# A decoder block's output projection as seven products of blocks instead of eight, in a second pass over all tokens

## The chip, the cores and the metric

The kernel runs on one core of a Trainium2 chip. The time is the device time of one execution in microseconds (us); the number compared is a median over runs.

## The reference

The kernel computes a whole hybrid decoder block for 2048 tokens of width 1024 behind 16 learned meta tokens: a norm, one wide input projection, gated linear attention, latent attention, two branch projections, a gated merge, and the output. Only the end matters here:

```python
        y_b = (o_b * jax.nn.silu(m_z)) @ mla_proj[l]

        merged = jax.nn.sigmoid(gate_gla) * y_a + jax.nn.sigmoid(gate_mla) * y_b
        h = h + merged @ w_out[l]
    out = rms_norm(h, final_norm_g)
    return out[:, N_META:]
```

`y_a` times its gate is stored earlier in the kernel as `ma`. All values are float32. A product in float32 is made of three products of parts: each operand is split into hi (a rounded copy, made by ScalarE) and lo (operand less hi), and hi x hi, hi x lo and lo x hi are summed in PSUM by `mm3` (lines 44 to 47).

## The kernel before

The engines are TensorE (PE; PEld is its weight load), VectorE (DVE), ScalarE (ACT), GpSimd (POOL) and SyncE (SP), from whose queue all the transfers start. The program is written with a tile framework: pools of buffers are opened on the left or right end of SBUF, a tile waits for a buffer of its pool and tag, and the framework orders the instructions of each engine by when it takes them to be ready and, among those, by their place in the program. So the order in the trace isn't quite that of the text.

The stages are: the input projections (`phase_ab`, which already makes most of them by seven products of blocks for eight), the linear attention between them, the branch projection of the linear attention (`GlaProj`), the latent attention (`phase_c`) and the class `Output` (line 1530), which ends the kernel.

`Output` works in eight rounds `t` of 256 tokens. A round has two halves.

The merge: for each `mo` of eight blocks of 128 output columns, eight `kc` times three products of 128x256 go to `acc` (`product`, line 1562). They take `wp_hi`, `wp_lo` (columns `m` of `mla_proj`, loaded in round 0 by `load_w` in two halves of 256 KB through two raw buffers, split by `load_columns`, and kept) and `ob_hi`, `ob_lo` (attention output, transposed; `load_ob`, line 1577, loads each piece `kc` through one of two raw buffers, ACT rounds it, POOL subtracts). There are 12 buffers of each of these parts, 8 in use. ACT makes the sigmoid of a gate piece `gm` in three steps, DVE multiplies `acc` by it and adds `ma`, and the sum is split into `mg_hi`, `mg_lo`.

The projection: for each of two blocks of 128 tokens and each half of the 1024 columns, eight `kc` times three products of 128x512 go to `oacc`, from the round's `mg` parts and the parts of `w_out` (`wo_hi`, `wo_lo`, loaded and split in round 0 by `load_wo`, line 1601, and kept). DVE adds the row block of `x`, ACT squares with a sum, `rsqrt_cols` gives the scale and DVE scales both halves, which SP stores.

The first two `mo` of round 0 (`first`, line 1552) already run beside the end of the latent attention, with weights and `ob` loaded by `early` (line 1545); that end is the transposes `p_tp` of attention rows, the sums `o_acc` and a last product `po`. The rest of the weights of both kinds arrive during round 0. `main` opens its pools of weights `d_wb` and pieces `d_io` on the left end, where the latent attention held its constants, those of `po` among them; its rows and transposed parts lay on the right end.

## Time and profile before

| | us |
|---|---|
| median of 3 runs | 2585.53 |
| lowest, highest | 2579.38, 2586.53 |
| the profiled execution, its own time | 2587.8 |
| its span, first to last instruction | 2586.1 |
| mean granted clock of TensorE, as a share of 2.4 GHz | 0.996 |

The profile is of one execution. A page of it lists the busy time of each engine; windows give the same for chosen stretches, in us from the span's start; groups by line give counts, busy time and the mean duration of one instruction; timelines give single instructions: start, duration, engine, line, operation, output<-inputs, shape, count, and in brackets the idle time before it and what ended that. The duration of a matmul reaches from its start to the modelled end of its results, and neighbours overlap; the distance of two starts is the pace.

### The profile page before, as it was taken

How to read it: one execution, taken by the hardware profiler on the slowest of the kernel's cores; microseconds unless marked ns; L12 is line 12 of the kernel's file. 1: busy time of each engine (PE TensorE's matmuls, PEld its weight loads, DVE VectorE, ACT ScalarE, POOL GpSimd, SP SyncE). 2: the span in 40 equal slices, each digit the busy share in tenths (PEclk: the TensorE clock that was granted, in tenths of full speed). 3: DMA queues.
4: the chain of work that ended last, by engine and by line, in shares of the span. 5: the costliest groups of instructions: out<-in, count | busy, mean ns of one | idle time of the engine just before them, and what ended most of it. 6: DMA issues, size and time to landing. Idle time of an engine off the chain costs nothing.

```text
span 2586.1 us, 42507 instructions
## 1 busy us (share of the span) xinstructions
PE 2523.7 (98%) x14873; PEld 2234.2 (86%) x14873; DVE 1604.6 (62%) x3910; ACT 1343.8 (52%) x3202; POOL 325.4 (13%) x333
## 2 busy tenths in 40 slices
PE   7999999999999999999999999999999999899998
PEld 7998887878998888888877889999999999799997
DVE  7435878887624477786432387777776666543433
ACT  5323555774523275575354476655555555644342
POOL 2102332221301100000000010000000000211010
PEclk9999999999999999999999999999999999999999
DMA  5556776777466877777674332211111100643432
GB/s 145 164 158 230 254 243 208 245 243 238 116 185 208 247 227 243 242 238 231 225 231 146 111 119 67 65 46 42 46 38 34 33 18 25 195 150 115 126 109 70
DMA packets 302086, 392.59 MB, mean 152 GB/s; under 512 B 40464, under 2 KB 218944, under 8 KB 301872
## 3 DMA queue, kind: packets, MB, share of 16 engines
q1 hardware_dynamic: 301872, 389.88, 47.7%
q8 instruction: 117, 1.92, 0.3%
q14 instruction: 97, 0.79, 0.1%
HBM read 240.51 MB, written 149.25 MB: 151 GB/s over the span
## 4 chain that ended last, share of the span: by engine, by line
PE 75%; DVE 8%; ACT 7%; DMA 6%; issue 2%; POOL 2%; SPq 0%; DVEq 0%; POOLq 0%; ACTq 0%
PE acc L47 12%; PE acc L46 12%; PE acc L45 12%; PE p_tp L1383 4%; PE o_acc L46 3%; PE o_acc L45 3%; PE o_acc L47 3%; PE s L1331 2%; PE s L1335 2%; PE s L1333 2%; PE s L1334 2%; PE s L1332 2%; PE oacc L47 2%; PE oacc L46 2%; PE oacc L45 2%
## 5 line engine op out<-in xcount | busy, mean ns | idle before, releaser
L45 PE MATMUL acc<-t_hi,xp 128*128 128x512 f32 x640 | 254.6, 398 | 0.8 <-DVE y_lo L1120 0.8
L47 PE MATMUL acc<-t_hi,xp 128*128 128x512 f32 x640 | 250.3, 391 | 0.0
L46 PE MATMUL acc<-t_lo,xp 128*128 128x512 f32 x640 | 249.9, 390 | 0.0
L47 PE MATMUL acc<-w_hi,y_lo 128*128 128x296 f32 (+1 forms) x640 | 193.9, 304 | 4.8 <-DVE y_lo L187 4.8
L46 PE MATMUL acc<-w_lo,y_hi 128*128 128x296 f32 (+1 forms) x640 | 194.5, 304 | 3.3 <-DVE w_lo L187 3.0
L45 PE MATMUL acc<-w_hi,y_hi 128*128 128x296 f32 (+1 forms) x640 | 194.7, 305 | 2.5 <-ACT y_hi L186 1.6
L45 PE MATMUL acc<-y_hi,xp 128*128 128x512 f32 x480 | 192.0, 400 | 0.0
L47 PE MATMUL acc<-y_hi,xp 128*128 128x512 f32 x480 | 188.1, 392 | 0.0
L1350 ACT ACTIVATE row<-row,nm,sr 128x144 f32<-128x144 f32 (+15 forms) x128 | 167.3, 1307 | 39.6 <-DVE nm L1349 39.2
L46 PE MATMUL acc<-y_lo,xp 128*128 128x512 f32 x480 | 187.5, 391 | 0.0
L1386 DVE TENSOR_TENSOR p_lo<-p_tp,p_hi 128x512 fp32r<-128x512 f32 x224 | 150.3, 687 | 49.3 <-ACT p_hi L1385 46.6
L1385 ACT ACTIVATE p_hi<-p_tp 128x512 fp32r<-128x512 f32 x224 | 129.5, 595 | 98.3 <-PE p_tp L1383 97.5
L1383 PE MATMUL p_tp<-ident,row 128*128 128x128 f32 x1088 | 168.4, 273 | 0.0
L1337 DVE TENSOR_SCALAR_CACHE_REDUCE row<-s 128x388 f32<-128x388 f32 (+13 forms) x224 | 130.9, 585 | 59.4 <-PE s L1335 57.3
L45 PE MATMUL acc<-ob_hi,wp_hi 128*128 128x256 f32 x504 | 141.7, 281 | 3.8 <-ACT wp_hi L1092 2.9
L47 PEld LDWEIGHTS acc<-t_hi,xp 128*128 128x128 f32 x640 | 120.1, 188 | 25.8
L45 PEld LDWEIGHTS acc<-t_hi,xp 128*128 128x128 f32 x640 | 120.5, 188 | 24.5 <-issue 1.8
L47 PE MATMUL acc<-ob_hi,wp_lo 128*128 128x256 f32 x504 | 141.0, 280 | 0.1
L1383 PEld LDWEIGHTS p_tp<-ident,row 128*128 128x128 f32 x1088 | 128.8, 140 | 14.3 <-ACT row L1350 4.6
L46 PE MATMUL acc<-ob_lo,wp_hi 128*128 128x256 f32 x504 | 140.9, 280 | 0.0
L1331 PE MATMUL s<-kt_hi,q_hi 128*128 128x420 f32 (+16 forms) x352 | 139.5, 397 | 1.2 <-DVE mx L1340 1.2
L46 PEld LDWEIGHTS acc<-t_lo,xp 128*128 128x128 f32 x640 | 120.4, 188 | 22.2
(338 smaller groups left out, 7293.5 us busy)
## 6 DMA issues: line engine op xcount, KB each, us to landing
d_xp<-xp SPq DMA_DIRECT2D x80, 512.0 KB
xp<-d_xp SPq DMA_DIRECT2D x80, 512.0 KB
w_raw<-in_w_in SPq DMA_DIRECT2D x60, 512.0 KB
xt<-in_x SPq DMA_DIRECT2D x32, 512.0 KB
d_z<-c SPq DMA_DIRECT2D x32, 256.0 KB
z<-d_z SPq DMA_DIRECT2D x64, 128.0 KB
v_hi<-d_vh SPq DMA_DIRECT2D x64, 128.0 KB
v_lo<-d_vl SPq DMA_DIRECT2D x64, 128.0 KB
```

What stands on the lines that cost most here:

```text
L45: nc.tensor.matmul(out, a_hi, b_hi, start=start, stop=False)
L46: nc.tensor.matmul(out, a_hi, b_lo, start=False, stop=False)
L47: nc.tensor.matmul(out, a_lo, b_hi, start=False, stop=stop)
L1331: nc.tensor.matmul(sv, q_hi[:, js], kt_hi[:, a:b], start=True, stop=False)
L1332: nc.tensor.matmul(sv, q_hi[:, js], kt_lo[:, a:b], start=False, stop=False)
L1333: nc.tensor.matmul(sv, q_lo[:, js], kt_hi[:, a:b], start=False, stop=False)
L1334: nc.tensor.matmul(sv, qa[:, js], kst[:, a:b], start=False, stop=False)
L1337: nc.vector.tensor_scalar(row[:, a:b], sv, 1.0, None, op0=ALU.mult, op1=ALU.max, accum_out=mx[:, i:i + 1])
L1350: nc.scalar.activation(row[:, :w], row[:, :w], AF.Exp, bias=nm, scale=sr[:, 4 * t + j:4 * t + j + 1], accum_out=rl[:, j:j + 1])
L1383: nc.tensor.transpose(tp[:, i, r * P:(r + 1) * P], rws[r][:, M + k * P:M + (k + 1) * P], ident)
L1385: nc.scalar.activation(fl(p_hi), fl(tp), AF.Copy)
L1386: nc.vector.tensor_sub(fl(p_lo), fl(tp), f(fl(p_hi)))
```

## The change

The output stage becomes two passes over all the tokens. The first, `merge`, runs the merge of all eight rounds; merged values aren't split but stored to a new DRAM tensor `S.mg`, one store for each piece of 128x256, issued one `mo` later. The pools `d_wb` and `d_io` now open on the right end, `ma` has four buffers of its own. In rounds 1 to 4 the generator `blocks` loads the rows `kc` and `4 + kc` of `w_out`, forms the sums t1 to t4 of its four blocks (DVE and POOL) and splits y11, t1, t2, t3 and y21 into parts that stay in SBUF; t4 goes to DRAM. From round 5 pools for the operands of the second pass are open, and in the last round `ahead` makes the first three operands.

The second pass, `project`, runs over eight pairs of row blocks of 128 tokens. For each pair, `operands` loads the merged values in halves of both dimensions and forms seven operands (four of them by a sum or difference, two made by DVE, two by POOL), each split by ACT and DVE into one of four buffers. Seven products of four `kc` times three matmuls of 128x512 follow, with the right sides y11, t1, t2, t3, y21, t4, y22. Out of PSUM, ACT copies the first and DVE adds the others to the four quarters of the two output rows; POOL adds the quarters of `x`; ACT squares; `finish` scales and the stores follow one step later. t4 and y22 are loaded and split at the start of the second pass.

```diff
+        self.mg = [pool.tile([P, KC, 512], F32, name=f"d_mg{t}") for t in range(NT)]
+        self.t4 = pool.tile([P, KC // 2, 512], F32, name="d_t4")
...
+    def merge(self):
...
+        wb = self.right("d_wb", KC - 1)
+        io = self.right("d_io", 3)
+        mp = self.right("d_mg", 4)
...
+        self.T = {n: [tp.tile([P, KH, 512], F32R, name=f"o{n}_{e}") for e in ("hi", "lo")]
+                  for n in ("y11", "t1", "t2", "t3", "y21")}
...
+        tmp = Pools(self.tc)
+        self.wraw, self.sums = tmp("d_wr", 1), tmp("d_ws", 1)
+        stores = []
...
+            build = self.blocks(t - 1) if 0 < t <= KH else None
+            if t == KH + 1:
+                tmp.close()
+                self.operands_pools()
...
+                while len(stores) > 1:
+                    nc.sync.dma_start(*stores.pop(0))
...
-                mg.append(self.split(hp, ma, ("mg_hi", "mg_lo"), nc.vector))
...
-                    for kc in range(KC):
-                        hi, lo = mg[kc]
-                        mm3(nc, acc[n], hi[:, bs], lo[:, bs], wo[kc][0][:, ns], wo[kc][1][:, ns],
-                            kc == 0, kc == KC - 1)
-                    nc.vector.tensor_add(xt[:, ns], xt[:, ns], acc[n])
-                    nc.scalar.activation(y[:, ns], xt[:, ns], AF.Square, accum_out=ssq[:, n:n + 1])
...
+                stores.append((S.mg[t * W // 512][:, mo, t * W % 512:t * W % 512 + W], ma))
+                if build is not None and mo % 2:
+                    next(build, None)
+                if t == last and mo >= 2:
+                    self.ahead()
...
+    def halves(self, n, kc, src, lo_engine):
+        hi, lo = self.T[n]
+        self.nc.scalar.activation(hi[:, kc], src, AF.Copy)
+        lo_engine.tensor_sub(lo[:, kc], src, f(hi[:, kc]))
+    def blocks(self, kc):
+        nc, KH = self.nc, KC // 2
+        up, dn = (self.wraw.tile([P, D], F32, tag=n, name=n) for n in ("w_up", "w_dn"))
+        nc.sync.dma_start(up, self.wo[kc * P:(kc + 1) * P])
+        nc.sync.dma_start(dn, self.wo[(KH + kc) * P:(KH + kc + 1) * P])
+        y11, y12, y21, y22 = up[:, :512], up[:, 512:], dn[:, :512], dn[:, 512:]
+        t1, t2, t3, t4 = (self.sums.tile([P, 512], F32, tag=f"f{i}", name=f"f{i}") for i in range(4))
+        yield
+        nc.vector.tensor_sub(t1, y12, y11)
+        nc.vector.tensor_sub(t2, y22, t1)
+        nc.gpsimd.tensor_sub(t3, t2, y11)
+        nc.gpsimd.tensor_sub(t4, y21, t2)
+        self.halves("y11", kc, y11, nc.vector)
+        yield
+        self.halves("t1", kc, t1, nc.vector)
+        self.halves("t2", kc, t2, nc.vector)
+        yield
+        nc.sync.dma_start(self.S.t4[:, kc], t4)
+        self.halves("t3", kc, t3, nc.vector)
+        self.halves("y21", kc, y21, nc.vector)
+    def operands_pools(self):
+        xp, self.mraw, self.msum = self.left("o_x", 3), self.left("o_raw", 1), self.left("o_sum", 1)
+        self.xps, self.made = [xp] * 3, 0
+        self.ops, self.ready = self.operands(), []
+    def operands(self):
+        nc, KH = self.nc, KC // 2
+        def load(p, k):
+            raw = self.mraw.tile([P, KH, 2 * P], F32, tag=f"r{k}", name="m_raw")
+            nc.sync.dma_start(raw, self.S.mg[p // 2][:, k * KH:(k + 1) * KH, p % 2 * 2 * P:(p % 2 + 1) * 2 * P])
+            return raw[:, :, :P], raw[:, :, P:]
+        def parts(src):
+            t = self.xps[self.made % len(self.xps)].tile([P, 2, KH, P], F32R, tag="xp", name="xp")
+            self.made += 1
+            nc.scalar.activation(t[:, 0], src, AF.Copy)
+            nc.vector.tensor_sub(t[:, 1], src, f(t[:, 0]))
+            return t
+        def summed(tag, eng, op, a, b):
+            t = self.msum.tile([P, KH, P], F32, tag=tag, name=tag)
+            eng.tensor_tensor(t, a, b, op=op)
+            return t
+        for p in range(L // (2 * P)):
+            x11, x21 = load(p, 0)
+            x12, x22 = load(p, 1)
+            yield parts(x11)
+            s1 = summed("sa", nc.vector, ALU.add, x21, x22)
+            yield parts(s1)
+            s2 = summed("sb", nc.vector, ALU.subtract, s1, x11)
+            yield parts(s2)
+            yield parts(summed("sa", nc.gpsimd, ALU.subtract, x11, x21))
+            yield parts(x12)
+            yield parts(x22)
+            yield parts(summed("sa", nc.gpsimd, ALU.subtract, x12, s2))
...
+    def ahead(self):
+        if len(self.ready) < 3:
+            self.ready.append(next(self.ops))
+    def project(self):
+        nc, KH, NP = self.nc, KC // 2, L // (2 * P)
+        right = Pools(self.tc, "right")
+        tp, xo, op = right("o_t", 1), right("o_in", 4), right("o_row", 4)
+        yo, up, sm, cst = right("o_y", 3), right("o_u", 1), right("o_sm", 6), right("o_cst", 1)
+        wr = right("o_wr", 4)
+        self.xps.append(right("o_x2", 1))
+        for n in ("t4", "y22"):
+            self.T[n] = [tp.tile([P, KH, 512], F32R, name=f"o{n}_{e}") for e in ("hi", "lo")]
...
+        def product(right):
+            acc = self.pb.tile([P, 512], F32, tag="b", name="oacc")
+            while len(self.ready) < 4:
+                t = next(self.ops, None)
+                if t is None:
+                    break
+                self.ready.append(t)
+            t = self.ready.pop(0)
+            hi, lo = self.T[right]
+            for kc in range(KH):
+                mm3(nc, acc, t[:, 0, kc], t[:, 1, kc], hi[:, kc], lo[:, kc], kc == 0, kc == KH - 1)
+            return acc
+        def step():
+            now = [s for s in stores if s[0] <= 0]
+            stores[:] = [(n - 1, *s) for n, *s in stores if n > 0]
+            for _, dst, src in now:
+                nc.sync.dma_start(dst, src)
+            if later:
+                later.pop(0)()
+        def finish(p, h, o, ssq):
+            nc.vector.tensor_add(ssq[:, :1], ssq[:, :1], ssq[:, 1:])
+            rstd = rsqrt_cols(nc, sm, ssq[:, :1], 1, 1.0 / D)
+            y = yo.tile([P, D], F32, tag="y", name="y")
+            r0 = (2 * p + h) * P
+            for n in range(2):
+                ns = slice(n * 512, (n + 1) * 512)
+                nc.vector.scalar_tensor_tensor(y[:, ns], o[:, ns], rstd, fg[:, ns], op0=ALU.mult, op1=ALU.mult)
+                stores.append((1, self.out[r0:r0 + P, ns], y[:, ns]))
...
+            nc.scalar.activation(c11, product("y11"), AF.Copy)
+            step()
+            p5 = product("t1")
+            step()
+            u2 = up.tile([P, 512], F32, tag="u2", name="u2")
+            nc.vector.tensor_add(u2, product("t2"), c11)
+            nc.vector.tensor_add(c12, p5, u2)
+            nc.gpsimd.tensor_add(c11, c11, x11)
+            nc.gpsimd.tensor_add(c12, c12, x12)
+            step()
+            nc.vector.tensor_add(c21, product("t3"), u2)
+            nc.vector.tensor_add(c22, p5, c21)
+            nc.gpsimd.tensor_add(c21, c21, x21)
+            nc.gpsimd.tensor_add(c22, c22, x22)
+            if p + 1 < NP:
+                xs[p + 1] = rows(p + 1)
+            step()
+            nc.vector.tensor_add(c11, product("y21"), c11)
+            square(0, 0, c11)
+            square(1, 1, c22)
+            step()
+            nc.vector.tensor_add(c21, product("t4"), c21)
+            square(1, 0, c21)
+            later.append(lambda a=(p, 1, o[1], ssq[1]): finish(*a))
+            step()
+            nc.vector.tensor_add(c12, product("y22"), c12)
+            square(0, 1, c12)
+            later.append(lambda a=(p, 0, o[0], ssq[0]): finish(*a))
+            if p + 1 < NP:
+                step()
...
```

## Rows read from the trace of the kernel before

**Rows 1.** The page's list of engines: busy time, share of the span, instructions.

```profile
PE 2523.7 (98%) x14873; PEld 2234.2 (86%) x14873; DVE 1604.6 (62%) x3910; ACT 1343.8 (52%) x3202; POOL 325.4 (13%) x333
```

**Rows 2.** Windows by stage: busy time of each engine (x instructions), columns in first line.

```profile
core 0: us, PE busy (x) PEld busy (x) DVE busy (x) ACT busy (x) POOL busy (x), PEclk, DMA share, GB/s
2218.40:2256.61 38.21, 32.06 (x197) 26.20 (x198) 23.36 (x35) 27.11 (x56) 11.14 (x10) 1.00 0.81 248
2256.61:2268.60 11.99, 10.55 (x46) 8.07 (x46) 9.28 (x17) 8.20 (x24) 4.08 (x4) 1.00 0.64 198
2489.76:2512.46 22.70, 22.70 (x194) 22.65 (x194) 11.82 (x30) 11.20 (x31) 1.54 (x2) 1.00 0.41 122
2512.46:2534.26 21.80, 21.80 (x98) 18.02 (x98) 5.70 (x14) 6.13 (x17) 1.55 (x3) 1.00 0.25 79
...
2578.53:2586.10 7.57, 0.00 (x0) 0.00 (x0) 3.05 (x9) 1.13 (x4) 0.00 (x0) 0.75 0.19 69
```

**Rows 3.** Groups by line, end of the kernel: count | busy us, mean ns | idle.

```profile
L46 PE MATMUL oacc<-wo_lo,mg_hi 128*128 128x512 f32 x256 | 99.8, 391 | 0.0
```

**Rows 4.** Timeline of PE, first and last of 20 products in a row.

```profile
2485.06 0.39 PE L45 MATMUL oacc<-wo_hi,mg_hi 128*128 128x512 f32 x1
...
2489.37 0.39 PE L46 MATMUL oacc<-wo_lo,mg_hi 128*128 128x512 f32 x1
```

**Rows 5.** Timeline of SP's queue: weight loads of gla_proj, then of mla_proj.

```profile
1290.38 2.36 SPq L1080 DMA_DIRECT2D w_raw<-in_gla_proj  x2
...
1302.82 1.85 SPq L1080 DMA_DIRECT2D w_raw<-in_gla_proj  x2
...
2219.84 1.61 SPq L1080 DMA_DIRECT2D w_raw<-in_mla_proj  x2
...
2253.08 1.88 SPq L1080 DMA_DIRECT2D w_raw<-in_mla_proj  x2
```

**Rows 6.** Timelines of PE and ACT around the first merge.

```profile
2212.80 0.49 PE L1383 MATMUL p_tp<-ident,row 128*128 128x128 f32 x3
...
2217.97 0.40 PE L47 MATMUL po<-och,wv_lo 128*128 128x512 f32 x1
...
2218.46 1.15 ACT L1092 ACTIVATE wp_hi<-w_raw 128x512 fp32r<-128x512 f32 x2 [1.34 <-PE po L47]
...
2256.33 0.28 PE L47 MATMUL acc<-ob_hi,wp_lo 128*128 128x256 f32 x1
```

**Rows 7.** Timelines of ACT, SP, PE and POOL around one end of a merge.

```profile
2466.16 0.71 ACT L1568 ACTIVATE ob_hi<-ob 128x256 fp32r<-128x256 f32 x2
...
2467.40 1.20 SPq L1581 DMA_DIRECT2D ob<-d_ob  x2
...
2468.02 0.40 PE L45 MATMUL oacc<-wo_hi,mg_hi 128*128 128x512 f32 x1
...
2471.51 0.74 POOL L1569 TENSOR_TENSOR ob_lo<-ob,ob_hi 128x256 fp32r<-128x256 f32 x1 [0.46 <-ACT ob_hi L1568]
```

**Rows 8.** Timelines of POOL and DVE in the paired input projections.

```profile
211.63 1.30 POOL L432 TENSOR_TENSOR sb<-sa,w_raw 128x512 f32<-128x512 f32 x1
...
211.91 1.57 DVE L187 TENSOR_TENSOR xp<-w_raw,xp 128x512 fp32r<-128x512 f32 x1
...
515.38 0.69 DVE L187 TENSOR_TENSOR xp<-w_raw,xp 128x512 fp32r<-128x512 f32 x1 [1.27 <-ACT xp L186]
515.99 0.69 DVE L522 TENSOR_TENSOR u<-acc,c 128x512 f32<-128x512 f32 x1
...
521.17 1.30 POOL L432 TENSOR_TENSOR sa<-w_raw 128x512 f32<-128x512 f32 x1 [8.65 <-DVE xp L187]
...
521.54 0.42 DVE L827 TENSOR_TENSOR kt_lo<-kt,kt_hi 128x256 fp32r<-128x256 f32 x1
```

**Rows 9.** Windows of the paired projections, columns as in rows 2.

```profile
472.00:493.50 21.50, 21.27 (x114) 18.06 (x113) 20.41 (x48) 18.40 (x49) 4.96 (x5) 1.00 0.71 234
...
536.50:558.00 21.50, 20.35 (x106) 16.88 (x105) 18.68 (x41) 15.17 (x42) 4.47 (x4) 1.00 0.76 247
```

**Rows 10.** Timeline of DVE behind the last product.

```profile
2581.66 1.41 DVE L1652 SCALAR_TENSOR_TENSOR y<-xt,rs_y,fg 128x512 f32<-128x512 f32 x2
```

More of the change, by code (lines that the diff above doesn't have):

```diff
@@ L1586, in main @@
     def main(self):
+        self.merge()
+        self.project()
+        self.left.close()
+        self.psum.close()
+        self.psum_r.close()
+    def merge(self):
         nc, S, W = self.nc, self.S, self.W
         self.obp += [self.right("d_ob2", 4)] * 4
-        left, psp = self.left, self.psum
-        wb = left("d_wb", KC - 1)
-        io = left("d_io", 3)
-        hp = left("d_h", 10)
-        cst = left("d_cst", 1)
-        xo = left("d_x", 2)
-        sm = left("d_sm", 3)
-        self.pa.append(psp("d_pa2", 2, space=PSUM))
-        pb = psp("d_pb", 4, space=PSUM)
-        fg = cst.tile([P, D], F32, name="fg")
-        wo = []
-        def load_wo(kc):
-            if kc == 0:
-                nc.sync.dma_start(fg, self.fg.partition_broadcast(P))
-            raw = xo.tile([P, D], F32, tag="x", name="wo_raw")
-            nc.sync.dma_start(raw, self.wo[kc * P:(kc + 1) * P])
-            wo.append(self.split(cst, raw, (f"wo_hi{kc}", f"wo_lo{kc}"), nc.vector))
+        wb = self.right("d_wb", KC - 1)
+        io = self.right("d_io", 3)
+        mp = self.right("d_mg", 4)
+        tp = self.left("d_t", 1)
+        KH = KC // 2
+        self.T = {n: [tp.tile([P, KH, 512], F32R, name=f"o{n}_{e}") for e in ("hi", "lo")]
+                  for n in ("y11", "t1", "t2", "t3", "y21")}
+        self.pa.append(self.psum("d_pa2", 2, space=PSUM))
+        self.pb = self.psum("d_pb", 4, space=PSUM)
+        tmp = Pools(self.tc)
+        self.wraw, self.sums = tmp("d_wr", 1), tmp("d_ws", 1)
+        stores = []
+        last = L // W - 1
         for t in range(L // W):
```

60 lines of the change are left out of this document (37 added, 23 removed).

## The prediction

> **What bounds the kernel now.** The page's list of engines comes first: TensorE (PE) is busy for 98% of the span [rows 1], so only work taken off PE, or waits put on it, can count. The windows by stage then show which part of the output stage is full [rows 2]. In a later round the merge takes 22.70 us and the output projection 21.80 us, PE busy throughout; DVE is at about half in the one and a quarter in the other, DMA at 0.41 and 0.25. The start differs: from 2218.40 to 2256.61 PE is busy for 32.06 of 38.21 us and DMA share is 0.81. The list by line has 768 products into oacc, 256 on each of three lines [rows 3]. Their mean there is latency, not pace; the timeline gives the pace: 19 starts in 4.31 us, 0.2268 us each [rows 4].
>
> **What is removed.** Eight products of blocks become seven: 8 pairs x 7 x 4 x 3 = 672 products for 768. The 96 saved are worth 96 x 0.2268 = 21.8 us, one round's projection.
>
> Where does that leave the end? Before, first-round projection ends at 2268.60 and last at 2578.53: seven rounds, 309.9 us. Afterwards, what follows the first merge is seven merges and 672 products (152.4 us), again seven times 22.70 + 21.80. So the gain equals how much earlier the first merge is through than 2268.60, less new waits. In the kernel before its last product starts at 2256.33 [rows 6]; after it 12.0 us of projection remained [rows 2], the other 9.8 us having filled holes between arriving weights. With the first merge unchanged the gain is 12.0 us, not 21.8: the filler is lost.
>
> **The first merge.** It is paced by columns of mla_proj: two loads for each m, issued from 2219.84 to 2253.08, five intervals of 6.65 us [rows 5]. w_out's eight 512 KB loads no longer run among them. The nearest row without such company is the same loader on gla_proj, two intervals in 12.44 us, 6.22 each [rows 5]. From m=3 to m=7 are four intervals: 4 x 0.43 = 1.7 us earlier. Bounds: nothing, since blocks of w_out for round 1 may load early too, and 1.7.
>
> The chain's start may move. The first split of these weights waited for product po, begun last at 2217.97 [rows 6], as d_wb lay over attention constants on the left; on the right it lies over attention rows and parts, whose last transposes start at 2212.80 [rows 6]. Between 0 and 2218.46 - 2213.3 = 5.2 us; I take 2, since some of those parts are read until shortly before po.
>
> For filler PE has only round 1's first products. Four ob pieces can be ahead (12 slots, 8 in use): 12 products of 256 columns, 22.70 / 192 = 0.118 us each, 1.4 us for one accumulator and 5.6 for four. I take 1.4.
>
> Sum so far: 12.0 + 1.7 + 2.0 + 1.4 = 17.1 us.
>
> **What is added.** *Round boundaries, seven.* Pieces 4 to 7 of the next ob need slots that free only in the last mo. Their loads, split and POOL subtraction were hidden by the projection; now the next merge follows at once. In a boundary of before, the merge ended at 2468.02, the first two of these splits began at 2466.16, the next two loads at 2467.40, and the last subtraction, 0.74 us, at 2471.51 [rows 7]: 4.2 us after the end. PE needs that piece after 22 products, 2.6 us. So 1.7 us with no filler, and nothing if PE takes the next mo's pieces 0 to 5 first, as it filled holes in the start. I take 0.7 each, 5 us, bounds 0 and 11.9. SP queues other loads behind those that wait for a raw buffer; three gm and four ma buffers give the merge about 8 us of cover.
>
> *Through DRAM.* Merged values are stored and loaded, 1 MiB a round each way, with their waits on SP. A merge round then moves 4 MiB in 22.7 us, 185 GB/s, and 5.25 MiB, 243 GB/s, in the four rounds with blocks; the start ran at 248 [rows 2]. Cost nothing while a load has a buffer ahead; otherwise it appears in the boundaries above, which is why I don't take 0 there.
>
> *Making the sums.* Blocks of rounds 1 to 4 add 7 DVE operations of 0.69 us [rows 8], 5 ACT copies and 2 POOL subtractions to a round; DVE's 11.82 us of a merge [rows 2] rise by 4.8 at most (the splits of merged values leave), under PE's 22.70. Without that cover they would add some 5 us a round.
>
> *Handover.* Three operands are ready; t4 and y22, loaded and split after the merge pools close, are wanted after five and six products of 12 x 0.2268 = 2.72 us, 13.6 us later. I take 1 us, bounds 0 and 3 (a product).
>
> *The projection pass.* A pair takes 84 x 0.2268 = 19.05 us of PE. DVE does 7 splits, 2 sums and 7 additions from PSUM, spaced 0.60 us where DVE is full (515.38 to 515.99) [rows 8], 9.6 us; four scalings, 1.41 us for two [rows 10], 2.8; and 12 small operations of 0.16 to 0.2, 2.3: 14.7 us, 77%. POOL does 6 additions of 1.30 us, 7.8 [rows 8]. These collide: while POOL ran 1.30 us from 211.63, a DVE split with both inputs in SBUF, 0.69 us otherwise, took 1.57; a DVE subtraction from PSUM under the POOL row of 521.17 took its usual 0.42 [rows 8]. So only splits, sums, scalings and the small multiplications, some 9.2 us, exclude POOL. If half of POOL's six each cost DVE 0.9 us, DVE is at 17.4 of 19.05 us, 91%. In stretches of 21.5 us with DVE at 20.41 and 18.68, PE lost 0.23 and 1.15 [rows 9], but those wait on a recurrence too; four operands ahead cover about 8 us here. I take 0.2 a pair, 1.5 us; bounds 0 and, if nothing overlaps (22.5 us a pair), 28.
>
> The Trainium skill, "SBUF — State Buffer", section "Who interferes with whom", says that a DVE instruction with two SBUF inputs and a GpSimd one that reads SBUF shut each other out for a whole instruction. The trace agrees, 1.57 us for 0.69, and 0.42 where an input is in PSUM [rows 8]. By that rule alone a pair lies between 17.0 us, which leaves the sum as it is, and 22.5 us, the second rival.
>
> ACT has some 8 copies (two in 1.15 us [rows 6]) and four squares a pair, under 10 us of 19, costed at nothing.
>
> *End.* After the last product 7.57 us remain [rows 2]; the same chain stays, with the other row block's scaling beside it: 0.8 us, bounds 0 and 2.
>
> **Sum.** 17.1 - 5 - 1 - 1.5 - 0.8 = 8.8 us. The profiled execution took 2587.8 us (span 2586.1), so it would take 2579.0; the median of the three runs, 2585.53, is 2.3 below that execution, giving 2576.7 us.
>
> **Rivals.**
> 1. *Boundaries are not filled.* PE's order keeps mo after mo, so seven waits of 1.7 us stay: 17.1 - 11.9 - 3.3 = 1.9 us, 2583.6. Slower loads in a fuller DMA would take it to about 2592. For: nothing but the next mo can fill, and DMA nearly doubles. Against: in the start PE did take out-of-turn products whenever weights were late. 22%.
> 2. *VectorE and GpSimd bound the projection pass: slower.* Place: the 6 POOL additions a pair against splits and scalings. Price: up to 22.5 - 19.05 = 3.45 us a pair, 28 us in all; 17.1 - 6.8 - 28 = -17.7, 2603. It decides once POOL costs DVE over 4.3 us a pair (14.7 + 4.3 = 19.05), and turns the whole change slower at about 5.6. For: 0.9 to 1.1 us in single collisions. Against: 4.2 us of PSUM additions a pair can run beside POOL. 9%.
> 3. *A quick first merge.* Chain 5.2 us earlier, four accumulators of filler, boundaries filled: 12.0 + 1.7 + 5.2 + 5.6 - 1 = 23.5, 2562. 17%.
> That fewer products are not issued isn't open: the loops fix 672.
>
> **How the numbers follow.** The forecast has 52%, with 2570 to 2582 as its own range. Range for 8 in 10: 2563 (rival 3) to 2592 (rival 1's far end); rival 2 and part of rival 3 lie outside. A measurement here tells about 0.3%, 7.8 us, from no change, so the line is 2577.8. Faster: 37 of the forecast's 52 and rival 3's 17, 54%. Same: 15 from the forecast and 18 from rival 1, 33%. Slower: 4 from rival 1 and rival 2's 9, 13%.
>
> **What would show it.** Right: 672 products into oacc at 0.227 us; first merge through at about 2250; seven merges in 158 to 165 us with small PE gaps only at boundaries, ended by ob_lo or ob_hi; pairs of 19 to 19.3 us; 8 us behind the last product. Wrong: PE gaps of over 2 us at boundaries (rival 1); DVE over 95% in the projection pass with PE waiting for xp (rival 2); first merge before 2246 (rival 3) or after 2257, which would undo the first terms.

## The result, and the profile after

The changed kernel takes 2624.14 us (median of four runs, 2622.8 to 2625.3), the kernel before 2584.46 us beside it: a ratio of 1.0156, 95% interval 1.0139 to 1.0174. It is slower by 40 us, where 2576.7 us had been forecast with a range of 2563 to 2592. The profiled execution has a span of 2623.3 us against 2586.1, so 37.2 us are to be found.

The page's list of engines, after [rows 1]:

```profile
PE 2528.3 (96%) x14777; PEld 2235.0 (85%) x14777; DVE 1660.4 (63%) x3970; ACT 1368.0 (52%) x3222; POOL 409.6 (16%) x389
```

96 products fewer, and PE is busy 4.6 us longer. Windows by stage (columns as the first line says): rest of the first merge, seven merges, projection pass, tail [rows 2].

```profile
core 0: us, PE busy (x) PEld busy (x) DVE busy (x) ACT busy (x) POOL busy (x), PEclk, DMA share, GB/s
2218.40:2250.50 32.10, 23.49 (x157) 21.82 (x158) 10.50 (x21) 18.48 (x42) 10.46 (x10) 0.89 0.70 207
2250.50:2448.20 197.70, 177.45 (x1337) 170.66 (x1336) 78.89 (x146) 98.47 (x240) 55.13 (x60) 0.93 0.58 181
2448.20:2612.80 164.60, 156.34 (x674) 125.38 (x672) 121.98 (x244) 65.18 (x158) 67.99 (x47) 1.00 0.47 154
2612.80:2623.30 10.50, 0.01 (x1) 0.00 (x0) 5.14 (x17) 2.18 (x8) 0.00 (x0) 0.69 0.27 101
```

The second line holds the result: seven merges take 197.7 us, where 158 to 165 were forecast, and the granted clock, 1.00 in every stage of [rows 2] that had products, is 0.93 over these 198 us. Against the terms of the forecast:

| stage | forecast | measured | late by |
|---|---|---|---|
| first merge through (the first round's projection was, before: 2268.60) | 2250 | 2250.5 | 0 |
| seven merges | 158 to 165 (309.9 - 152.4 = 157.5, and 5 for boundaries) | 197.7 | 35 |
| handover and 672 products | 154.9 (152.4 + 1 + 1.5) | 164.6 | 10 |
| behind the last product | 8.4 | 10.5 | 2 |

From the kernel before: -18.1 + 40.2 + 12.2 + 2.9 = 37.2 us, the difference in span.

PE's waits after 2250 us (line waiting, what it waited for: us in total, times, longest):

```profile
PE acc L45 <- ACT ob_hi L1574: 11.1, 8, 2.5
PE oacc L45 <- ACT xp L1695: 8.1, 6, 1.5
PE acc L46 <- POOL ob_lo L1575: 7.9, 15, 1.5
PE acc L45 <- ACT wp_hi L1094: 0.8, 1, 0.8
PE oacc L47 <- DVE xp L1696: 0.2, 1, 0.2
```

In the merges nearly all of them are for pieces of the next round's ob. The 40.2 us can be split by the distance from one product's start to the next, less a product's pace of 0.118 us. Distances over 0.5 us are waits, 25.1 us. Distances near 0.213 us, half the clock, make some 9 us. Those of 0.3 to 0.5 us, in which short waits and half the clock mix, make 4 us, and a pace of 0.120 in place of 0.118 makes the remaining 2.4. By boundary, from the first to the seventh, the loss is 4, 11, 6, 8, 5, 2 and 4 us; the sums are made in the merges that end at the second to the fifth. Windows behind the second boundary and the fourth, and at the seventh, columns as above:

```profile
2283.00:2287.00 4.00, 2.00 (x8) 1.49 (x7) 3.67 (x4) 3.17 (x8) 3.40 (x3) 0.50 0.53 167
2287.00:2291.00 4.00, 3.07 (x15) 2.78 (x14) 2.13 (x3) 2.72 (x7) 2.70 (x3) 0.50 0.54 184
...
2347.00:2351.00 4.00, 4.00 (x20) 4.00 (x21) 1.50 (x3) 3.01 (x8) 2.55 (x3) 0.56 0.73 217
2351.00:2355.00 4.00, 4.00 (x36) 4.00 (x35) 0.98 (x3) 1.01 (x3) 0.47 (x1) 1.00 0.65 191
...
2424.00:2428.00 4.00, 1.31 (x6) 0.91 (x7) 0.00 (x0) 2.35 (x6) 1.46 (x2) 1.00 0.61 192
```

After the waits of the first five boundaries the granted clock falls to 0.50, the level of 1.2 GHz, for 27 us in all; at the sixth and seventh it stays at 1.00, although PE is busy for 1.31 of 4 us in the last line. In the line from 2347 PE is busy throughout at 0.56 and starts 20 products, where the next line, at 1.00, starts 36. So the clock cost between 9 us, the starts 0.213 us apart, and 13 us with the mixed ones.

How a boundary comes late, from the timelines of SP, POOL, ACT and PE at the second one, the end of the first of the seven merges:

```profile
2262.04 0.40 SPq L1631 DMA_DIRECT2D ma<-d_ma  x1
...
2264.65 1.75 POOL L1668 TENSOR_TENSOR f<-w_dn,f 128x512 f32<-128x512 f32 x1
...
2266.43 0.32 SPq L1674 DMA_DIRECT2D d_t<-f  x1
...
2268.24 0.42 SPq L1628 DMA_DIRECT2D gm<-d_gm  x1
...
2271.66 0.42 ACT L134 ACTIVATE gm<-gm 128x256 f32<-128x256 f32 x1 [4.34 <-DMA gm<-d_gm]
...
2272.43 0.40 ACT L1574 ACTIVATE ob_hi<-ob 128x256 fp32r<-128x256 f32 x1
...
2274.50 2.40 SPq L1587 DMA_DIRECT2D ob<-d_ob  x2
...
2276.56 0.63 ACT L1653 ACTIVATE oy_hi<-w_up 128x512 fp32r<-128x512 f32 x1 [0.82 <-DMA w_up<-in_w_out]
...
2279.02 0.71 ACT L1574 ACTIVATE ob_hi<-ob 128x256 fp32r<-128x256 f32 x2
...
2279.47 0.38 PE L45 MATMUL acc<-ob_hi,wp_hi 128*128 128x256 f32 x1 [2.06 <-ACT ob_hi L1574]
2279.50 1.60 POOL L1575 TENSOR_TENSOR ob_lo<-ob,ob_hi 128x256 fp32r<-128x256 f32 x2 [2.94 <-ACT ob_hi L1574]
```

SP stands from 2262.4 to 2266.4 at the store of t4, until POOL has made it; gm is requested late; ACT stands 4.34 us at that gm, and ob's rounding is behind it. The next requests of ob wait for one of two raw buffers (2.40 us for two requests), and ACT stands at w_up. In every queue something stands ahead of ob's pieces, so there is a candidate in each: SP, ACT, POOL, two raw buffers. Which of them was it?

### The profile page after: what moved, and what is told of

Same layout as the page of the kernel before. It is cut to its first block, busy times and chain, and to the rows that moved or that the text cites. A ratio compares the mean times of both kernels' runs of the same rounds, so it can differ in the third digit from the quotient of the medians.

```text
span 2623.3 us, 42759 instructions
## 1 busy us (share of the span) xinstructions
PE 2528.3 (96%) x14777; PEld 2235.0 (85%) x14777; DVE 1660.4 (63%) x3970; ACT 1368.0 (52%) x3222; POOL 409.6 (16%) x389
## 4 chain that ended last, share of the span: by engine, by line
PE 63%; DVE 11%; DMA 10%; ACT 7%; issue 5%; POOL 3%; SPq 1%; POOLq 0%; DVEq 0%; ACTq 0%
PE acc L46 11%; PE acc L47 11%; PE acc L45 11%; PE p_tp L1385 4%; PE o_acc L46 3%; PE o_acc L45 3%; PE o_acc L47 2%; PE s L1333 2%; PE s L1337 2%; PE s L1335 2%; PE s L1336 2%; PE s L1334 2%; DMA ob<-d_ob 1%; DMA m_raw<-d_mg 1%; DMA gm<-d_gm 1%
## 5 line engine op out<-in xcount | busy, mean ns | idle before, releaser
L1339 DVE TENSOR_SCALAR_CACHE_REDUCE row<-s 128x388 f32<-128x388 f32 (+13 forms) x224 | 130.9, 585 | 59.4 <-PE s L1337 57.3
L45 PE MATMUL acc<-ob_hi,wp_hi 128*128 128x256 f32 x504 | 149.2, 297 | 19.1 <-ACT ob_hi L1574 11.1
L46 PE MATMUL acc<-ob_lo,wp_hi 128*128 128x256 f32 x504 | 149.8, 298 | 8.2 <-POOL ob_lo L1575 7.9
L47 PE MATMUL acc<-ob_hi,wp_lo 128*128 128x256 f32 x504 | 147.4, 294 | 1.6 <-POOL wp_lo L1095 1.4
L1438 POOL TENSOR_TENSOR rb<-rb,mz 128x512 f32<-128x512 f32 x32 | 42.0, 1313 | 644.2 <-DMA rb<-d_rl 337.9
```

Source lines behind the costliest of these rows:

```text
L45: nc.tensor.matmul(out, a_hi, b_hi, start=start, stop=False)
L46: nc.tensor.matmul(out, a_hi, b_lo, start=False, stop=False)
L47: nc.tensor.matmul(out, a_lo, b_hi, start=False, stop=stop)
L1339: nc.vector.tensor_scalar(row[:, a:b], sv, 1.0, None, op0=ALU.mult, op1=ALU.max, accum_out=mx[:, i:i + 1])
```

## The experiments

The names: A, two raw buffers and 12 part buffers; B, POOL; C and E, SP's queue; D, the sums of w_out's blocks; G, ob's pieces as a whole; F and H are told with their runs. The table gives, for each profiled execution, the merges (from the last product of po to the last product into acc, since the stage starts at 2213 to 2221 us), the pass from there to the last product into oacc, and the time as a whole. By the kernel before's rows the merges would be 38.4 us for the first [rows 6] and seven times 22.70 [rows 2], 197.3. Kernels whose merges are the changed kernel's show 229.4, 233.3 and 234.3 us: the framework orders them anew each time, and up to 5 us mean nothing. The kernel before was timed beside each kernel, with medians of 2584.5 to 2588.7 us, so times are better compared by the last column.

| kernel | merges | pass | time | ratio to before, interval |
|---|---|---|---|---|
| the changed kernel | 229.4 | 164.4 | 2624.1 | 1.0139 to 1.0174 |
| four raw buffers | 223.1 | 163.8 | 2618.6 | 1.0107 to 1.0143 |
| ob asked for earlier | 230.2 | 164.7 | 2625.4 | 1.0133 to 1.0173 |
| sums on VectorE | 225.8 | 165.5 | 2622.0 | 1.0120 to 1.0160 |
| sums later in the text | 233.2 | 165.4 | 2632.0 | one run |
| t4 stored later | 229.1 | 164.7 | 2627.0 | 1.0135 to 1.0165 |
| t4 later, four raw buffers | 223.3 | 165.9 | 2614.0 | 1.0086 to 1.0120 |
| sums behind the merges | 218.1 | 199.5 | 2647.6 | one run |
| stores from ScalarE's queue | 239.7 | 164.4 | 2633.5 | 1.0162 to 1.0194 |
| stores from GpSimd's queue | 235.8 | 163.7 | 2624.5 | 1.0127 to 1.0161 |
| six ma buffers | 230.5 | 166.0 | 2624.6 | 1.0133 to 1.0166 |
| ob loaded once | 199.3 | 171.3 | 2603.8 | one run |
| sums in half steps | 230.8 | 166.2 | 2622.1 | one run |
| half steps, 16 part and 4 raw buffers | 222.5 | 165.3 | 2614.0 | 1.0097 to 1.0131 |
| the same, second r1 | 222.8 | 161.0 | 2610.5 | 1.0079 to 1.0109 |
| the same, five gm buffers | 231.1 | 161.2 | 2619.5 | 1.0104 to 1.0138 |
| ob once, sums behind the merges | 190.8 | 206.7 | 2628.3 | one run |
| second r1 | 233.3 | 162.5 | 2623.0 | 1.0124 to 1.0158 |
| second r1, no additions of x | 234.3 | 155.2 | 2617.5 | 1.0102 to 1.0136 |

**Single links of the boundary.** First the raw buffers:

```
-        self.obr = self.right("d_obr", 2)
+        self.obr = self.right("d_obr", 4)
```

> Four raw buffers for the pieces of ob in place of two; nothing else changes. Theory A (the eight pieces of the next round come through two raw buffers, two at a time, and each pair waits until the pair before has been split): all of a round's first pieces can be under way before the boundary, so PE's waits between 2250 and 2448 us fall from 25.1 us to 8 or less, the stretches at half the granted clock that follow them from 13.7 to 5 or less, and the time falls by 20 to 32 us, to 2592 to 2604. Rival B (GpSimd: its subtraction for each piece stands behind the sums of w_out's blocks, which are on GpSimd too): no more raw data helps, the time falls by less than 5 us. Rival C (SP's queue: the requests stand behind stores and loads that wait on SP): the requests leave no earlier for a free buffer, less than 8 us.

5.5 us, not 20 to 32; that is rival C's range. The requests did leave early: from the third boundary on all eight pieces were asked for 6 to 29 us before the round's last product started. PE's waits for ob were still 16.1 us, of 19.0. A loaded piece also needs one of 12 part buffers, and that was left as it was. Next the order of the requests:

```
-            ob = self.obs if t == 0 else self.load_ob(t)
+            ob = self.obs if t == 0 else ahead + self.load_ob(t, range(KH, KC))
...
+                if mo == 5 and t < last:
+                    ahead = self.load_ob(t + 1, range(KH))
```

> Two raw buffers as in the changed kernel, but the first four pieces of a round's ob are requested and split in the round before, ahead of its sixth product, and only the last four at the boundary. Theory A: four of eight pieces are in place at the boundary, the other four make two trips through the two buffers beside the first of the products; the waits fall to 10 us or less and the time by 18 to 30 us, to 2594 to 2606. Rival B (GpSimd held by the sums): the four rounds with sums keep their waits of 4 us or more each, the time falls by 10 us or less. Rival C (SP's queue): falls as by A, since the requests now stand ahead of the stores that wait; A and C are told apart by the kernel with four raw buffers, which leaves the queue's order alone.

Nothing, but the run tells little, since in its trace the requests hardly moved: only at the second and third boundary do the first four pieces mostly leave earlier, by up to 8 us; from the fourth on some leave a little earlier and some later. What speaks against A as it was put, eight pieces through two raw buffers at the boundary, is the changed kernel itself: from the third boundary on it asks for at least six of the eight ahead of the round's last product. GpSimd's part of the sums:

```
-        nc.gpsimd.tensor_sub(t3, t2, y11)
-        nc.gpsimd.tensor_sub(t4, y21, t2)
+        nc.vector.tensor_sub(t3, t2, y11)
+        nc.vector.tensor_sub(t4, y21, t2)
```

> The two sums of w_out's blocks that GpSimd computes (t3 and t4, 8 instructions of 1.7 us in rounds 2 to 5) go to VectorE; nothing else changes. Theory A: GpSimd's subtractions for ob are shorter in four of seven rounds, but the trips through two buffers stay: the time falls by 0 to 6 us. Rival B: the boundaries of those four rounds, which cost some 7 us each, come down to the 3.3 us of the later ones, and the clock with them: 15 us or more faster.

2 us, less than these runs can tell, so B falls. The store that SP stood at, alone and with four raw buffers:

```
-        nc.sync.dma_start(self.S.t4[:, kc], t4)
+        self.late = (self.S.t4[:, kc], t4)
...
+            if 1 < t <= KH + 1:
+                nc.sync.dma_start(*self.late)
```

> The store of t4 (one in each of the four rounds with sums) is issued on SP at the start of the next round, when GpSimd has long made t4; nothing else changes. Theory D: SP no longer stands some 4 us a round at that store (2262.4 to 2266.4 in the first), gm, ma and ob are requested that much earlier, and the four rounds lose 2 to 5 us less each: the time falls by 8 to 20 us, to 2604 to 2616. Theory A: the trips through two raw buffers stay, the time falls by 4 us or less.

> The store of t4 later, as in the kernel before this one, and four raw buffers for ob. If both hold in turn (with four buffers alone, 5.5 us were gained, since SP then issued no earlier): more than the two gains together, 20 to 35 us, to 2589 to 2604. If they are independent: their sum, 12 to 20 us. If neither is the cause: 6 us, as with four buffers alone.

Nothing alone, although the 4 us stand of the timeline is gone (3.4 us at two later stores stay). The stall that looked worst in the timeline was covered by the next link in the row. Both together gave 10 us, but the interval overlaps that of four raw buffers alone, and the merges are as long, 223.3 and 223.1 us. SP's other stands in the merges are at ob's raw buffers (25.0 us), at the stores (26.7) and at buffers of ma that a store still holds (26.3):

```
-                    nc.sync.dma_start(*stores.pop(0))
+                    nc.scalar.dma_start(*stores.pop(0))
```

> The 64 stores of the merged blocks are issued from ScalarE's queue in place of SP's; nothing else changes. Theory E: SP's 26.7 us at the stores go, and the requests of gm, ma and ob leave earlier: the seven merges take 172 to 188 us in place of 198, the time falls by 10 to 26 us, to 2598 to 2614. Rival F (the in-order queue of whichever engine issues the store stands as long, and on ScalarE the splits and gates stand behind it): 4 us or less, or slower by up to 20 us. Theory A (two raw buffers alone): no change.

> The same 64 stores from GpSimd's queue. Theory E: as with ScalarE's, 2598 to 2614. Rival F: GpSimd's subtractions for ob stand behind the stores that wait for VectorE, the waits of PE move from ScalarE's part of ob to GpSimd's, and the time stays within 4 us or gets worse by up to 20 us.

```
-        mp = self.right("d_mg", 4)
+        mp = self.right("d_mg", 6)
```

> Six buffers for ma in place of four (a buffer now holds its block until the store has landed, where the kernel before split it in SBUF); nothing else changes. Theory E: SP's 26.3 us at the requests of ma go, the requests behind them leave earlier: the time falls by 6 to 16 us, to 2608 to 2618. Theory A (ob's two raw buffers): 3 us or less. Theory D (the sums): 3 us or less.

Slower from ScalarE's queue, as rival F said, by 9 us, or 6 against the kernel before beside it; no difference from GpSimd's or with six buffers. None of this speaks for theory E, but it doesn't rule it out either: SP's stand at buffers of ma grew to 62.4 and 59.4 us in the first two, and in the third it fell to 22.6 only, with 29.3 at the stores.

**Whole causes.** The sums were taken out of the merges, first in the text only:

```
-            build = self.blocks(t - 1) if 0 < t <= KH else None
+            build = None
...
+        for kc in range(KH):
+            for _ in self.blocks(kc):
+                pass
```

> The four steps that build the sums of w_out's blocks leave the merges of token blocks 2 to 5 and run after the last merge, with nothing beside them; the two raw buffers and the order of everything else stay. The time as a whole gets worse by 20 to 60 us, since PE stands during these steps; the question is how long the seven merges take, from the eighth ma addition of one to that of the next (in the changed kernel 33.0, 31.5, 32.7, 26.4, 28.3, 24.5 and 26.4 us, where the products alone need 22.7). Theory D (the steps of the sums hold SP, ScalarE and VectorE in their order of issue: SP stands at the store of t4 until GpSimd has made it, ScalarE at w_up's and w_dn's loads, and the requests and splits of ob behind them come late): the first four come down to 23 to 26 us each, 20 to 30 us less in all. Theory A (two raw buffers for ob alone, as in the rounds without sums): the first four come down only to 26 to 28 us each. Rival B (GpSimd alone): as by D, but then GpSimd's subtractions were what moved.

This told nothing of D: in its trace the sums stand in the merges all the same, ACT's first split of w_up at 2264.53, since the framework starts what it takes to be ready. With their buffers where the last merge's ob had been, they could not:

```
+        self.right.close()
+        tmp = Pools(self.tc, "right")
+        self.wraw, self.sums = tmp("d_wr", 1), tmp("d_ws", 1)
```

> The steps that build the sums of w_out's blocks are really moved behind the last merge: their buffers now lie where the merges' last parts of ob lay, so that the framework can't start them earlier (in the kernel that moved them in the text alone it still put them beside the merges). The time as a whole gets worse by 20 to 60 us; the question is how long the seven merges take (changed kernel: 198 us for the seven, 28 to 33 in the rounds with sums, 24.5 to 28 in those without; the products alone 22.7 each). Theory D (the sums hold SP, ScalarE and VectorE): all rounds come down to 23 to 25 us, the seven to 162 to 175 us. Theory E (SP's one queue: it stands at the stores of ma until VectorE has made them, and at the requests of ma until a store has left its buffer, 26 us each of the 198, and ob's requests stand behind): the rounds stay at 25 to 28 us, the seven at 178 to 195.

11 us less in the merges. The seven take 185.5 us (2250.0 to 2435.5), which is in theory E's range and not in D's: the sums are a part, and not the larger one. Then ob:

```
-            ob = self.obs if t == 0 else self.load_ob(t)
+            ob = self.obs
```

> Leaves out the loads and splits of ob for rounds 2 to 8: all eight rounds take round 1's pieces. Everything else (sums, gates, ma, stores, projection) stays. Theory G (the boundary's own chain: only four of a round's eight pieces can be ready, the others are loaded, rounded and subtracted one behind the other while PE waits, and the clock falls behind each wait): the seven merges take 158 to 168 us in place of 198, with hardly a wait of PE and the full clock, and the time is 2584 to 2596. Theories D and E (the sums, or SP's stores, hold the engines for whatever is behind): the waits move from ob to the gates and the accumulators; the merges still take 175 to 195 us.

30 us less in the merges, 167.5 us for the seven, as theory G said. The windows of this kernel while the sums were made and after, columns as before:

```profile
2252.70:2334.50 81.80, 74.89 (x603) 73.88 (x602) 47.15 (x81) 41.72 (x93) 15.96 (x10) 0.98 0.62 196
2334.50:2420.20 85.70, 85.70 (x716) 85.64 (x715) 24.69 (x59) 36.42 (x88) 0.00 (x0) 1.00 0.44 135
```

From 2334.5 on PE is busy throughout at its full clock. The time, 2603.8 us, is outside G's range: it fell by 20 us only, as the merges began 2 us later and the projection pass took 7 us more (171.3), with waits for operands and for y22's parts in its first two pairs. Before 2334.5 the sums show in waits for the accumulators, 6.2 us. The longest of them, from the timelines of ACT, DVE and PE:

```profile
2299.32 0.42 ACT L136 ACTIVATE gm<-gm 128x256 f32<-128x256 f32 x1
...
2301.72 0.69 DVE L1666 TENSOR_TENSOR f<-w_dn,f 128x512 f32<-128x512 f32 x1 [2.94 <-DMA w_dn<-in_w_out]
...
2304.60 0.41 DVE L1640 TENSOR_TENSOR gm<-acc,gm 128x256 f32<-128x256 f32 x1
...
2305.07 0.39 PE L45 MATMUL acc<-ob_hi,wp_hi 128*128 128x256 f32 x1 [3.42 <-DVE gm L1640]
```

The gate is ready at 2299.74, but DVE stands until 2301.72 for a load that a sum needs, then works on the sums until 2304.60, and only then empties the accumulator. Last, both out:

> Leaves out ob's loads and splits for rounds 2 to 8, as in the run before, and has the sums of w_out's blocks behind the last merge, as in the run that really moved them; both together. The time as a whole says nothing (the sums then stand alone at the end). Theory G with the sums (the 40 us are these two and nothing else; 28 went with ob alone and 11 with the sums alone): the seven merges take 158 to 164 us, all of them 22.5 to 24 us, with less than 3 us of waits in all. Theory E (SP's stores and loads of gm and ma bound a row of merges by themselves): waits of PE on the accumulators stay, 8 us or more in all, and the merges take 168 us or more.

Window of its seven merges, and SP's waits in it:

```profile
2252.70:2409.20 156.50, 156.50 (x1304) 156.50 (x1305) 48.72 (x111) 66.84 (x159) 1.72 (x1) 1.00 0.47 142
```

```profile
SPq L1628 <- DMA d_mg<-ma: 84.1, 51, 3.7
```

PE waits nowhere and has its full clock, 0.120 us a product, while SP stands 84 us at the requests of ma (line 1628), for buffers that a store still holds. So storing the merged values and SP's stands cost PE nothing by themselves, and the 39 us (229.4 - 190.8) are ob's pieces, 30, and the sums, 11, give or take the 5 us by which like kernels differ. This run has no requests of ob, so it doesn't show whether SP's stands delay them where they are there.

**Room for the parts.** Half steps for the sums free 8 KB; 16 part and four raw buffers fill it:

```
+        h = slice(e * 256, (e + 1) * 256)
...
-        t1, t2, t3, t4 = (self.sums.tile([P, 512], F32, tag=f"f{i}", name=f"f{i}") for i in range(4))
+        t1, t2, t3, t4 = (self.sums.tile([P, 256], F32, tag=f"f{i}", name=f"f{i}") for i in range(4))
...
+        ob3 = Pools(self.tc, "right")
+        self.obp += [ob3("d_ob3", 4)] * 4
```

> The sums of w_out's blocks are built in steps of half the columns (eight steps, each instruction half as long), in buffers half as large; ob as in the changed kernel. It is the ground for the two kernels after it. Theory G: the merges take 190 to 200 us as before, the time 2618 to 2628. Theory D (long steps of the sums in the engines' order): 8 us or more less.

> The half steps for the sums, and in the room that they free 16 buffers for the parts of ob in place of 12 (but 12 for the last round) and four raw buffers: all eight pieces of the next round can be split while the round before runs. Theory G: PE's waits at six of seven boundaries go, the seven merges take 165 to 178 us, the time falls by 20 to 32 us, to 2592 to 2604. Theory E (SP's queue) : requests still leave late, the merges take 180 us or more, the time falls by less than 15 us.

The half steps alone change nothing. With room for the parts PE's waits for ob go down, from 19.0 us to 5.9, but 10.5 us of waits for accumulators, of which the changed kernel's merges have none, take their place: the merges gain 7 us, and the time 10 for 20 to 32 expected. By the ranges set down for this run that is theory E's result (some 191 us for the seven merges, less than 15 us gained), though ob's requests left up to 40 us ahead. Timelines of ACT, DVE and PE of this kernel at the longest of those waits:

```profile
2392.71 0.42 ACT L136 ACTIVATE gm<-gm 128x256 f32<-128x256 f32 x1
...
2394.99 0.63 ACT L1700 ACTIVATE xp<-m_raw 128x512 fp32r<-128x512 f32 x1 [1.86 <-DMA m_raw<-d_mg]
2395.56 0.42 ACT L134 ACTIVATE gm<-gm 128x256 f32<-128x256 f32 x1
...
2395.65 0.69 DVE L1701 TENSOR_TENSOR xp<-m_raw,xp 128x512 fp32r<-128x512 f32 x1 [5.22 <-ACT xp L1700]
2396.26 0.42 DVE L1644 TENSOR_TENSOR gm<-acc,gm 128x256 f32<-128x256 f32 x1
...
2396.73 0.38 PE L45 MATMUL acc<-ob_hi,wp_hi 128*128 128x256 f32 x1 [3.57 <-DVE gm L1644]
```

The projection pass's first operand stands in the queues ahead of the merge's gate: DVE waits 5.22 us for a split that is wanted 40 us later, while the gate is ready from 2393.13 on, and the accumulators fill behind it. The Trainium skill, "PSUM — Partial Sum Buffer", section "Engine vs sequencer instructions", says that the queues of ScalarE, VectorE and GpSimd are strictly first in, first out; these rows agree. This is one wait of ten. The other nine, 7.0 us, come before the first operand; at the longest of them, 2.3 us up to 2319.9, DVE stands 6.30 us at w_up for a sum.

The next two kernels add a second r1, and then five gm buffers:

> As the kernel before this one, and a second buffer for r1 in the projection pass as in the run for it alone (which took 4 us of PE's waits out of that pass and put 3.5 us of others in). Theory G: 3 us or less faster than the kernel before it, 2588 to 2602: the pass stays bound by VectorE's additions.

> The kernel with half steps, 16 buffers for the parts of ob and a second r1, and now five buffers for gm in place of three (in that kernel PE's waits had moved from ob to the accumulators, 16.5 us, which VectorE empties only when gm's gate has come; ob's raw data come through the two weight buffers to make room). If gm's buffers are the next link: these waits fall to 6 us or less and the time by 8 to 16 us, to 2594 to 2602. If SP's order holds gm back: 4 us or less.

The second r1 is the best version of the change that was found, 2610.5 us, still 0.8 to 1.1% behind the kernel before. Five gm buffers made it worse: the waits for accumulators, counted from 2215 us on, grew from 16.5 to 21.0 us, and those for ob's rounding from 4.7 to 11.8. As that kernel also took ob's raw data through the weight buffers, it doesn't tell which of the two did it.

**The projection pass.** Timelines of SP, DVE, ACT and PE of the changed kernel at one of five like waits (2504.87 to 2588.72, 20.7 to 21.1 us apart, 7.9 us together):

```profile
2536.82 5.74 SPq L1771 DMA_DIRECT2D out_y<-y  x4
2542.86 0.38 SPq L1689 DMA_DIRECT2D m_raw<-d_mg  x1
...
2547.06 0.69 DVE L1701 TENSOR_TENSOR sa<-m_raw 128x512 f32<-128x512 f32 x1 [2.46 <-issue]
2547.86 0.63 ACT L1695 ACTIVATE xp<-sa 128x512 fp32r<-128x512 f32 x1 [5.70 <-DVE sa L1701]
2548.50 0.47 PE L45 MATMUL oacc<-oy_hi,xp 128*128 128x512 f32 x1 [1.48 <-ACT xp L1695]
```

The next pair's r1 is asked for behind four output stores that wait for DVE, into the only buffer for r1. A second pair of buffers, for both halves, had no room (8 KB a partition, 7.53 were left). So r1 alone got a second one:

```
+        self.mraw.append(right("o_raw2", 1))
...
-            raw = self.mraw.tile([P, KH, 2 * P], F32, tag=f"r{k}", name="m_raw")
+            raw = self.mraw[p % 2 if k and len(self.mraw) > 1 else 0].tile([P, KH, 2 * P], F32, tag=f"r{k}", name="m_raw")
```

> A second buffer for r1 alone (the halves of the merged blocks that are read second; 4 KB a partition) from the second pair of token blocks on; the merges stay as they are. Theory A for the projection pass (each pair's wait of 1.4 to 1.5 us ends the chain from r1's late load): the six waits and the slow stretches behind them go, the time falls by 7 to 12 us, to 2612 to 2617. Rival (VectorE's and GpSimd's additions and scalings bound the pass): 3 us or less, and PE's waits move to another instruction.

The five waits go, and four on DVE's additions come, 2.9 us; the pass falls by 2 us, a pair from 21.0 to 20.3. One early pair takes 23.2 us, with a wait for xp of 1.4 us and half the clock behind it. The new waits, from the timelines of POOL, DVE and PE at one of them:

```profile
2543.73 1.62 POOL L1804 TENSOR_TENSOR o_row<-o_row,x_in 128x512 f32<-128x512 f32 x1 [3.98 <-ACT xp L1695]
2544.71 1.18 DVE L1701 TENSOR_TENSOR sa<-m_raw 128x512 f32<-128x512 f32 x1
2545.30 1.74 POOL L1805 TENSOR_TENSOR o_row<-o_row,x_in 128x512 f32<-128x512 f32 x1
2545.92 1.67 DVE L1701 TENSOR_TENSOR sb<-sa,m_raw 128x512 f32<-128x512 f32 x1
2547.52 0.68 DVE L1807 TENSOR_TENSOR o_row<-oacc,u 128x512 f32<-128x512 f32 x1
...
2548.34 0.47 PE L45 MATMUL oacc<-oy_hi,xp 128*128 128x512 f32 x1 [0.74 <-DVE o_row L1807]
```

Under GpSimd's two additions DVE's sums of two SBUF operands take 1.18 and 1.67 us, and the addition that PE waits for is behind them. Then GpSimd's additions of x were left out too:

> As the kernel with a second buffer for r1, but it leaves out the additions of x (four on GpSimd for each pair of token blocks; x is loaded and not used). Theory H (once r1 comes in time, the pass is held by VectorE, whose additions and subtractions of two SBUF operands take 0.8 to 1.7 us beside GpSimd's in place of 0.69, 17.5 of 21 us busy): PE's four waits of 0.7 to 0.8 us on o_row go, a pair takes 19.1 to 19.6 us in place of 20.4, VectorE's busy time in 21 us falls to 15 to 16, and the time falls against that kernel by 5 to 9 us, to 2614 to 2618. Rival (the order of VectorE's queue and its own length hold the pass, not GpSimd): the waits stay, 2 us or less.

A window with the second r1 alone, and DVE's group for the splits of sums from 2480 to 2608 us (count | busy us, mean ns | idle):

```profile
2548.00:2569.00 21.00, 19.99 (x86) 16.05 (x87) 17.52 (x34) 7.97 (x20) 8.89 (x6) 1.00 0.52 158
```

```profile
L1696 DVE TENSOR_TENSOR xp<-sa,xp 128x512 fp32r<-128x512 f32 x19 | 17.3, 909 | 0.0
```

The same two views without the additions:

```profile
2548.00:2569.00 21.00, 21.00 (x93) 17.07 (x92) 16.38 (x38) 9.59 (x23) 2.58 (x2) 1.00 0.32 107
```

```profile
L1696 DVE TENSOR_TENSOR xp<-sa,xp 128x512 fp32r<-128x512 f32 x19 | 13.1, 687 | 0.3
```

PE has no wait in the last 576 products, and the pass takes 155.2 us, near the 152.4 of its products. DVE's splits come down from 909 to 687 ns and its busy time from 17.5 us to 16.4 in 21, with more products done in it. That is theory H. Not all of the 7 us between the two passes are its doing: the four waits make 3.6 us from start to start, and the early pair of 23.2 us, 20.3 here, makes another 3, for which no run shows the cause. The Trainium skill, "SBUF — State Buffer", section "Who interferes with whom", on two engines shutting each other out, agrees with these two rows as with [rows 8].

## Why the prediction was wrong

*What is removed* was right: 672 products into oacc, at 0.23 us.

*The first merge* came out as a sum, 18.1 us for 17.1, and partly by luck: the first merge was through at 2250.5, but two terms were off in opposite ways. From the loads of column m=3 to those of m=7 it took 21.8 us (2219.09 to 2240.88), where the kernel before took 27.3 (2219.84 to 2247.16): 5.5 us, where 1.7 was both the term and its bound. The start of the chain moved by 0.75 us, where 2 were taken.

*Round boundaries* is the step that failed: "I take 0.7 each, 5 us, bounds 0 and 11.9". Seven boundaries cost 30 us with ob's loads and splits in the merges, and nothing without. The waits were where the step put them, but not of its size. Three things were wrong in it. The 1.7 us were read from a boundary of the kernel before [rows 7], where each merge was followed by 21.80 us of projection in which SP, ACT and POOL could catch up; where merges follow one another there is no such stretch. The bound was set by the last link alone, the subtraction, with every other link on time; the runs show a row of links, where making one faster only lets the next be seen. And no price was put on the clock, which [rows 2] showed at 1.00 in stages where PE was never idle: 9 to 13 of the 40.2 us.

*Making the sums*, "under PE's 22.70", was costed at nothing by shares of busy time: some 11 us. DVE and ACT had the time, as forecast (78.89 and 98.47 of 197.7 us). What PE waited for was their place in the queues, where they stand for loads and work ahead of a gate that is ready, as in the rows at 2299 to 2305 us.

*Through DRAM*, "cost nothing while a load has a buffer ahead", held: with ob and the sums out of the way SP stood 84 us for buffers that the stores held, and PE not at all.

*Handover* was right, 0.12 us between the merges' last product and the first into oacc, and 1.2 us of waits a pair later. *The projection pass*, 1.5 us, measured 12: 9.4 us are PE's waits, from start to start, 7.9 of them for an r1 that has one buffer and stands behind output stores, a queue that the step didn't look at. The collision that it did look at comes into sight once that wait is gone, 2.9 us of waits, a tenth of the 28 us of rival 2, whose place was right and whose price was not reached.

*End*, 0.8 us, measured 2.9. Timeline of DVE behind the last product at 2612.42 [rows 10]:

```profile
2613.48 0.16 DVE L1776 TENSOR_TENSOR ssq<-ssq 128x1 f32<-128x1 f32 x1 [2.06 <-ACT jk L1794]
...
2614.99 0.68 DVE L1821 TENSOR_TENSOR o_row<-oacc,o_row 128x512 f32<-128x512 f32 x1
2615.59 1.41 DVE L1782 SCALAR_TENSOR_TENSOR y<-o_row,rs_y,fg 128x512 f32<-128x512 f32 x2
```

The other row block's small chain and its scaling stand in DVE's queue around the last addition, which starts 2.6 us after the last product.

Rival 1 named the place, boundaries that are not filled, and went to 2592; its price was low by 32 us, by the same step. What stays open is which link of ob's pieces weighs most. Each was tried alone and none gave over 6 us. Four raw buffers left 16.1 us of PE's waits for ob, and 16 part buffers beside them 5.9, so the part buffers were what held ob back once the requests were early; the merges gained only 7 to 8 us, since the waits moved to the accumulators. Whether SP's order holds the gates or ob back isn't shown, since no kernel with ob's loads shortened SP's stands much. Loads of ob from another queue weren't tried, nor a merge that doesn't share ACT's and DVE's queues with the sums and the pass's first operands.

## What to carry to other kernels

Work that stands between two stages of an interleaved loop hides the feeding of both; when stages of one kind are put in a row, give each its whole feed (loads, splits, gates, stores) in the shorter time, queue by queue and in order, before any saving is counted. Where several queues are late together, price the cause as a whole by leaving its input out before mending links one by one. And add the clock to every wait of PE: here a microsecond of waiting cost a third to a half of a microsecond more at half the clock.

## What the runs showed of the hardware

The granted clock fell to 0.50 within a row of six waits of 0.3 to 2.1 us, 5.7 us in all, between 2277 and 2289 us (PE busy for 2.00 and 3.07 of 4 us from 2283 to 2291), and was 0.56 from 2347 to 2351 us with PE busy throughout; yet it stayed at 1.00 at the seventh boundary, with PE busy for 1.31 of 4 us. SP could stand for 84 of 157 us in its queue with PE at full pace, so a large sum of waits in one queue is no measure of what it costs. Beside GpSimd's additions DVE's operations on two SBUF operands took 1.18 and 1.67 us and the splits 909 ns on average; without them the splits took 687 ns.
